# The shared key projection moved from the attention's first stage between the steps of a recurrence

## The chip, the cores and the metric

One core of a Trainium2 chip runs the whole program. Its engines work in parallel, each through its own queue in order: TensorE (PE) multiplies matrices, VectorE (DVE) and ScalarE (ACT) work on elements, GpSimd (POOL) does some of the same, SyncE (SP) mostly issues DMA transfers. ScalarE's queue issues transfers too. PSUM holds the results of TensorE, SBUF the operands, DRAM everything larger. The metric is the device time of one execution in microseconds, the median of several.

## The reference

A trunk of two layers over 2048 tokens of 1024 features. Layer 0 is a recurrence (RWKV-7) over time in 16 heads of 64. From its output, keys and values are computed once. Layer 1 is an attention with three groups of queries over these keys and values. Only the middle part changes here:

```python
xr = xr + gate * _rwkv7_time_mix(h, ...)                 # layer 0
kv = _rms(xr, kv_norm_g) @ w_kv                          # 1024 -> 2048
k_sh = kv[..., :D].reshape(B, S, N_HEADS, HEAD_DIM)
v_sh = kv[..., D:].reshape(B, S, N_HEADS, HEAD_DIM)
k_sh = _rope(_rms(k_sh, k_norm_g), cos, sin)             # norm and rotation of the keys
h = _rms(xr, b_norm_g[j]) * (1.0 + scale) + shift        # layer 1
xr = xr + gate * _dilated_mixer(h, k_sh, v_sh, ...)
```

All of it is float32.

## The kernel before

The kernel has three phases. The first (to about 1085 us) computes the projections of the recurrence. The second, called **the recurrence** here, goes over 32 chunks of 64 tokens. The third computes keys, values, queries and a gate in **jobs**, lets the attention run beside the later ones, and ends with the output projection.

A large product is made with three matmuls, because an operand in float32 is split into a high and a low half (`xh`, `xl` for tokens, `wh`, `wl` for weights): high x high, high x low, low x high. That is `mm3`, lines 72 to 74; `split` (lines 65 and 66) makes the halves of tokens, one on ScalarE and one on VectorE.

*The recurrence* (`phase2`). For each chunk, `loads` fetches the chunk's operands `ls`, `bk`, `tf`, `ut` and `x` on SP's queue (bk has one buffer), `prep` makes small triangular products from them (lines 881 to 913), and `chain` carries the state through three dependent sets of small matmuls (lines 942, 959 and 965), each of which waits for the evacuation of the one before. A chunk has ten slots; in each the program emits a step of the chain, one of `prep`, one of the chunk's normalization, and then fills from a list called `work`:

```python
fill(1, front)
fill(2 if len(work) > 1 and ch >= RUSH else 1)
```

Every block of 256 tokens (four chunks) pushes one `out_proj` onto that list: 38 steps, of which 32 hold 6 matmuls of 256 columns into the PSUM tile `pd` (192 of them), with `x1T` stored to DRAM and, at the end, the tokens' norm factor `rstd1`. `spread` ties each of these products to an earlier mark of the chain, so that a scheduler can't put them all ahead of it. The order in which each engine gets its instructions is set when the program is built, by that scheduler's own estimate of times.

*The jobs* (`phase3`, `project`). `JOBS = ("k", "v", 2, 1, 0, "gate", "out")`. A job goes over 8 blocks of 256 tokens (`tb`), and each block over 32 steps of one `mm3` with 512 columns, so 768 matmuls. `tokens` loads a tile of `x1T`, splits it, and in the value job also multiplies it by the norm (GpSimd, line 1314), modulates it (VectorE, line 1318) and stores it as `xbT` for the query jobs; the odd tiles of that job share two buffers (`yp`). `weight` loads and splits a weight tile, for keys and values with the factor `kv_norm_g` (lines 1282 and 1283). Behind every eighth step a result is taken out of PSUM: in the value job by `values_out` (scaled on ScalarE and stored), in the key and query jobs by `rotated`, which scales it on ScalarE (line 1444), norms and rotates it in `rms_rope` (VectorE lines 1205 to 1218, GpSimd lines 1207 and 1211), transposes it on PE (line 1450) and stores it, for the keys in two layouts, one of them in pieces of 64 bytes.

The attention starts when the first query job is done: `tick(256 * 3 + 14)` runs the three jobs k, v and 2 ahead of it.

## Time and profile before

| | |
|---|---|
| median of 3 runs | 3931.34 us (3910.43 to 3933.19) |
| the profiled execution | 3931.35 us, span 3929.6 us, mean granted clock 0.960 |
| PE busy | 3740.8 us, 95% of the span |
| VectorE, ScalarE, GpSimd busy | 64%, 46%, 36% |
| DMA | 595 MB, mean 151 GB/s |

The span runs from the first to the last instruction of the profile, the execution's time has a little around it. Busy shares of PE count a matmul from its start to its modelled end, and matmuls overlap, so a busy PE can still be slower than its peak. The granted clock is that of PE: 1.00 is 2.4 GHz and 0.5 is 1.2 GHz, and a figure between is a mean over a stretch.

### The profile page before, as it was taken

The numbers are of one execution on the slowest core, as the hardware profiler recorded it, in microseconds if no ns is written. First come the engines' busy times: TensorE is split into PE (matmuls) and PEld (weight loads), VectorE is DVE, ScalarE is ACT, GpSimd is POOL, SyncE is SP. The second block draws the span as 40 slices with busy tenths as digits, with TensorE's granted clock in tenths as the row PEclk, the third lists the DMA queues.
The fourth block names the chain that finished last, engine by engine and source line by source line (L and its number), as shares of the span: only waits on it lengthen the run. The fifth ranks groups of instructions, "written<-read, shape, count | busy, mean of one in ns | idle before, by whom it ended". The sixth has DMA issues, their size and how long they took to land. (4 is left out here: it accounts for less than half of the span.)

```text
span 3929.6 us, 79892 instructions
## 1 busy us (share of the span) xinstructions
PE 3740.8 (95%) x29328; PEld 2942.6 (75%) x29328; DVE 2501.7 (64%) x6212; ACT 1824.9 (46%) x4734; POOL 1430.3 (36%) x1376
## 2 busy tenths in 40 slices
PE   6899999989999999999898999899999999999999
PEld 5565667667778888888776877677777788887778
DVE  4884477989766565466575457777776654454545
ACT  4555444343334344344443233466666665564431
POOL 3341356664343344333343244533422320042232
PEclk9899999999978899899998999999999999999999
DMA  8774466675664444344588457855654455465555
GB/s 276 221 241 144 133 182 197 180 206 169 169 140 106 94 107 104 86 104 116 115 126 175 137 146 82 137 143 149 184 148 125 132 154 145 153 190 169 172 157 150
DMA packets 1027128, 595.31 MB, mean 151 GB/s; under 512 B 564912, under 2 KB 918576, under 8 KB 1020592
## 3 DMA queue, kind: packets, MB, share of 16 engines
q1 hardware_dynamic: 629040, 500.00, 45.6%
q10 hardware_dynamic: 397696, 90.20, 12.6%
q8 instruction: 232, 3.80, 0.4%
q14 instruction: 160, 1.31, 0.1%
HBM read 391.84 MB, written 198.18 MB: 150 GB/s over the span
## 5 line engine op out<-in xcount | busy, mean ns | idle before, releaser
L1645 ACT ACTIVATE yt<-yt,nm 128x256 f32<-128x256 f32 (+1 forms) x768 | 345.1, 450 | 320.0 <-DVE nm L1641 316.7
L72 PE MATMUL ps<-xh,wh 128*128 128x512 f32 (+1 forms) x1248 | 451.6, 372 | 11.5 <-ACT xh L358 7.7
L73 PE MATMUL ps<-xl,wh 128*128 128x512 f32 (+1 forms) x1248 | 449.6, 362 | 6.4 <-DVE xl L360 5.9
L74 PE MATMUL ps<-xh,wl 128*128 128x512 f32 (+1 forms) x1248 | 446.6, 359 | 0.0
L72 PE MATMUL ps<-xh 128*128 128x512 f32 (+1 forms) x1152 | 419.9, 365 | 5.9 <-ACT ov L1478 3.7
L74 PE MATMUL ps<-xh,xl 128*128 128x512 f32 (+1 forms) x1152 | 402.9, 350 | 0.0
L73 PE MATMUL ps<-xl,xh 128*128 128x512 f32 (+1 forms) x1152 | 400.9, 348 | 0.0
L1207 POOL TENSOR_TENSOR rr_st<-rr_st,mh 128x8 f32<-128x8 f32 x128 | 216.1, 1688 | 484.0 <-DVE rr_st L1206 340.6
L74 PE MATMUL ps<-wh,xl 128*128 128x512 f32 x896 | 360.2, 404 | 15.2 <-DVE xl L66 14.6
L72 PE MATMUL ps<-wh,xh 128*128 128x512 f32 x896 | 367.2, 411 | 3.4 <-ACT xh L65 1.8
L73 PE MATMUL ps<-wl,xh 128*128 128x512 f32 x896 | 359.3, 401 | 0.6 <-DVE wl L1283 0.5
L72 PEld LDWEIGHTS ps<-xh,wh 128*128 128x128 f32 x1248 | 239.4, 194 | 85.8 <-issue 34.3
L73 PEld LDWEIGHTS ps<-xl,wh 128*128 128x128 f32 x1248 | 241.7, 194 | 61.9 <-issue 19.2
L74 PEld LDWEIGHTS ps<-xh,wl 128*128 128x128 f32 x1248 | 241.8, 194 | 52.5 <-issue 21.4
L1638 DVE CUSTOM_DVE_ANT_0 yt<-sc,amask 128x256 f32<-128x256 f32 (+1 forms) x768 | 237.6, 359 | 66.3 <-PE sc L1633 60.5
L72 PEld LDWEIGHTS ps<-xh 128*128 128x128 f32 x1152 | 218.4, 190 | 54.9 <-issue 18.5
L74 PEld LDWEIGHTS ps<-xh,xl 128*128 128x128 f32 x1152 | 218.7, 190 | 29.0 <-issue 0.2
L73 PEld LDWEIGHTS ps<-xl,xh 128*128 128x128 f32 x1152 | 219.1, 190 | 25.1 <-POOL xl L1288 0.4
L1214 DVE TENSOR_TENSOR q<-rr_sq,TCS 128x256 f32<-128x256 f32 x256 | 223.4, 913 | 2.8
L1211 POOL TENSOR_TENSOR rr_a<-rr_sq,TCS 128x512 f32<-128x512 f32 x128 | 184.5, 1441 | 110.7 <-DVE rr_sq L1209 90.9
L278 DVE SCALAR_TENSOR_TENSOR t<-hx,vecs,t 128x512 f32<-128x512 f32 x192 | 169.4, 901 | 78.0 <-ACT t L277 77.6
L74 PEld LDWEIGHTS ps<-wh,xl 128*128 128x128 f32 x896 | 170.8, 191 | 62.7 <-DVE xl L66 26.5
(339 smaller groups left out, 8842.3 us busy)
## 6 DMA issues: line engine op xcount, KB each, us to landing
hx<-hT SPq DMA_DIRECT2D x152, 256.5 KB
xb<-xbT SPq DMA_DIRECT2D x256, 128.0 KB
x<-Q SPq DMA_DIRECT2D x96, 256.0 KB
kq<-K SPq DMA_DIRECT2D x72, 256.0 KB
st<-in_w_in SPq DMA_DIRECT2D x64, 256.0 KB
arD<-ar SPq DMA_DIRECT2D x32, 512.0 KB
bkD<-bk SPq DMA_DIRECT2D x32, 512.0 KB
ls<-arD SPq DMA_DIRECT2D x64, 256.0 KB
```

Of the source, the lines that this page charges most:

```text
L72: i = mm(out, lh, rh, start=first, stop=False, **kw)
L73: mm(out, lh, rl, start=False, stop=False, **kw)
L74: mm(out, ll, rh, start=False, stop=last, **kw)
L278: nc.vector.scalar_tensor_tensor(t1, hx[:, 0:512], self.vec["a_mix_mu"][:, m:m + 1], t1, op0=ALU.mult, op1=ALU.add)
L1207: nc.gpsimd.tensor_tensor(st[:, 1], st[:, 0], mh, op=ALU.pow)
L1211: nc.gpsimd.tensor_tensor(a, sq, TC[:, tt, None, :].to_broadcast([P, 8, 64]), op=ALU.mult)
L1214: nc.vector.tensor_tensor(v[:, :, lo:lo + 32], sq[:, :, hi:hi + 32], TS[:, tt, None, lo:lo + 32].to_broadcast([P, 8, 32]), op=ALU.mult)
L1638: nc.vector.tensor_tensor_reduce(out=u.pr[:, h, :nk], in0=sc[h][:, x, :nk], in1=amask[:, int(g == 0), 256 - nk:256], scale=1.0, scalar=-3e ...
L1645: nc.scalar.activation(u.pr[:, h, :nk], u.pr[:, h, :nk], AF.Exp, bias=nm[:, x, h:h + 1], accum_out=lm[:, x, h, 0:1])
```

## The change

The key job leaves the list of jobs. Its products are made in the recurrence: when an `out_proj` is done, it pushes a new generator `keys(v)` onto the same list `work`. It reads the block's 256 tokens back from `x1T`, splits them, and multiplies them by all 16 weight tiles of the keys (3 x 2 matmuls of 512 columns for each). The tiles don't stay in SBUF: the first block loads, scales and splits them and stores the halves to a DRAM scratch `wkD`; every later block reads both halves again, two tiles ahead, into three buffers. The result is scaled with `rstd1` on ScalarE and stored as `kraw`. A slot now fills two steps instead of one (three instead of two from chunk 24 on if the list is long).

In the third phase the value job comes first. Beside each of its 32 results the generator `rotated("k", ...)` now runs for the keys: it loads a tile of `kraw` in place of an evacuation and goes on as before. The value job's tokens, which were the second job's, keep their norm and modulation. The token pool of nine buffers is cut into one of five and one of four.

```diff
@@ phase2 @@
-            for n, bufs in (("wst", 2), ("dp", 1), ("op", 2)):
+            for n, bufs in (("wst", 2), ("dp", 1), ("op", 2), ("wk", 3)):
...
                 nc.gpsimd.tensor_tensor(self.rstd1[:, 2 * v:2 * v + 2], rs, mh[:, 0:2], op=ALU.pow)
+                push(keys(v))
+
+            def key_weight(v, i):
+                wh, wl = (late["wk"].tile([P, 512], F32R, name="wk" + x) for x in "hl")
+                if v:
+                    for x, t in enumerate((wh, wl)):
+                        nc.sync.dma_start(t.bitcast(F32), wkD[i, x])
+                    return lambda: (wh, wl)
+                kc, c = i % KC, i // KC * 512
+                st = late["wst"].tile([P, 512], F32, name="wst")
+                nc.sync.dma_start(st, ap["w_kv"][kc * P:(kc + 1) * P, c:c + 512])
+
+                def use():
+                    g = kvg[:, kc:kc + 1]
+                    nc.scalar.activation(wh, st, AF.Copy, scale=g)
+                    nc.vector.scalar_tensor_tensor(wl, st, g, wh.bitcast(F32), op0=ALU.mult, op1=ALU.subtract)
+                    for x, t in enumerate((wh, wl)):
+                        nc.sync.dma_start(wkD[i, x], t.bitcast(F32))
+                    return wh, wl
+                return use
+
+            def keys(v):
+                t0 = v * 256
+                xh = late["dp"].tile([P, KC, 2, P], F32R, name="yh").rearrange("p k i t -> p k (i t)")
+                xl = late["dp"].tile([P, KC, 2, P], F32R, name="yl").rearrange("p k i t -> p k (i t)")
+                uses = [key_weight(v, i) for i in range(2)]
+                for kc in range(0, KC, 4):
+                    nc.sync.dma_start(xl[:, kc:kc + 4].bitcast(F32),
+                                      self.x1T[kc * P:kc * P + 512, t0:t0 + 256].rearrange("(k p) t -> p k t", p=P))
+                yield
+                yield
+                for kc in range(0, KC, 2):
+                    q = slice(kc, kc + 2)
+                    raw = xl[:, q].bitcast(F32)
+                    nc.scalar.activation(xh[:, q], raw, AF.Copy)
+                    yielding(nc.vector.tensor_sub(xl[:, q], raw, xh[:, q].bitcast(F32)))
+                    yield
+                for half in range(2):
+                    ps = [late["pd"].tile([P, 512], F32, name="pd") for _ in range(2)]
+                    for kc in range(KC):
+                        i = half * KC + kc
+                        w = uses.pop(0)()
+                        if i + 2 < 2 * KC:
+                            uses.append(key_weight(v, i + 2))
+                        for b in range(2):
+                            c = slice(b * P, b * P + P)
+                            spread(self.mm3(ps[b], (xh[:, kc, c], xl[:, kc, c]), w, kc == 0, kc == KC - 1))
+                            yield
+                    for b in range(2):
+                        o = late["wst"].tile([P, 512], F32, name="wst")
+                        nc.scalar.activation(o, ps[b], AF.Copy, scale=self.rstd1[:, 2 * v + b:2 * v + b + 1])
+                        nc.sync.dma_start(self.kraw[t0 + b * P:t0 + b * P + P, half * 512:half * 512 + 512], o)
+                    yield
...
-                fill(2 if len(work) > 1 and ch >= RUSH else 1)
+                fill(3 if len(work) > 1 and ch >= RUSH else 2)
@@ phase3 @@
-            JOBS = ("k", "v", 2, 1, 0, "gate", "out")
+            JOBS = ("v", 2, 1, 0, "gate", "out")
...
+                if job == "k":
+                    nc.sync.dma_start(q, self.kraw[tt * P:tt * P + P, half * 512:half * 512 + 512].rearrange(
+                        "t (h c) -> t h c", c=64))
+                    for _ in range(4):
+                        yield
+                else:
+                    nc.scalar.activation(q, ps.rearrange("p (h c) -> p h c", c=64), AF.Copy)
...
+                        if job == "v" and kc == 0:
+                            after.append(rotated("k", tb * 2 + i, half, None))
...
-            tick(256 * 3 + 14)
+            tick(256 * 2 + 14)
```

The scheduler sets where the moved instructions stand. Counted in PE's order, the extra products of the four chunks of a block were 72, 60, 60 and none of 256 columns; in the changed kernel's steady pattern they are 120 of 256 columns, then 24 and 18 of 512, then 48 of 512, then 30 of 512 and 48 of 256. Behind the last chunk stand 252 of 256 columns before, and 192 of 256 with 174 of 512 now, the latter in part among 30 of the value job's.

PE's queue in the recurrence before, in a chunk without extra products, from the end of one block's norm on (`ls` and `tf` are operands of the chunk, `qc` an evacuated step of the chain, `bk` the next chunk's operand):

```order
L1093 MATMUL pd<-ones,acc 128x2 x2
L959 MATMUL ps<-qc_15992,tf_10366 64x64 x8
L881 MATMUL z<-ls_0_10355,bk 128x128 x4
L942 MATMUL ps<-x,ls_1_10362 64x64
L944 MATMUL y<-x,ls_1_10362 64x64
L942 MATMUL ps<-x,ls_1_10362 64x64 x7
```

The same place in the changed kernel (`wkh`, `wkl` are the halves of a key weight tile, `yh`, `yl` those of the tokens):

```order
L967 MATMUL ps<-x,ls_15454 64x64 x8
L1095 MATMUL pd<-ones,acc 128x2 x2
L969 MATMUL y<-x,ls_15454 64x64 x8
L72 MATMUL pd<-wkh,yh 128x512
L73 MATMUL pd<-wkl,yh 128x512
L74 MATMUL pd<-wkh,yl 128x512
```

Products of 512 columns follow where the chain's next set stood.

SP's queue in the recurrence before, loads of the next chunk (`x`, `ls`, `tf`) between those of the output projection:

```order
L1082 DMA x1T<-t_18533 128x256
L859 DMA tf_10359<-tdD 32x8x32 x4
L1074 DMA t_18995<-in_xT 128x256
L865 DMA x<-vP 64x512 x2
L850 DMA ls_1_10362<-arD 64x8x128 x2
```

In the changed kernel, while a block's keys are made:

```order
L867 DMA x<-vP 64x512 x2
L1108 DMA wkl<-wkD 128x512
L1108 DMA wkh<-wkD 128x512
L1154 DMA kraw<-wst 128x512
L852 DMA ls_0_10360<-arD 64x8x128
```

The load of `ls` now stands behind two weight halves and a store of finished keys.

VectorE's queue in the value job before (token splits on line 66, modulation on line 1318, weight halves on line 1288):

```order
L66 TENSOR_TENSOR xl<-yc,xh 128x256
L66 TENSOR_TENSOR xl<-xb,xh 128x256
L1318 TENSOR_SCALAR xb<-xb,gsB,adaB 128x256
L1318 TENSOR_SCALAR yc<-yc,gsB,adaB 128x256
L1288 TENSOR_TENSOR wl<-st,wh 128x512 x3
```

In the changed kernel (the modulation is now on line 1380, the keys' norm and rotation on lines 1264 to 1277):

```order
L1273 TENSOR_TENSOR q<-rr_sq,TCS 128x8x32 x2
L1277 TENSOR_TENSOR rr_a<-rr_a,q 128x512
L66 TENSOR_TENSOR xl<-yc,xh 128x256
L66 TENSOR_TENSOR xl<-xb,xh 128x256
L1264 TENSOR_REDUCE rr_st<-rr_sq 128x8
```

The splits now take turns with the rotation's instructions.

## Rows read from the trace of the kernel before

**Rows 1.** The page: busy us, share, instructions by engine; GB/s of 40 slices

```profile
PE 3740.8 (95%) x29328; PEld 2942.6 (75%) x29328; DVE 2501.7 (64%) x6212; ACT 1824.9 (46%) x4734; POOL 1430.3 (36%) x1376
...
GB/s 276 221 241 144 133 182 197 180 206 169 169 140 106 94 107 104 86 104 116 115 126 175 137 146 82 137 143 149 184 148 125 132 154 145 153 190 169 172 157 150
```

**Rows 2.** Windows: length; busy PE, PEld, DVE, ACT, POOL; clock, DMA share, GB/s

```profile
1840.00:1902.00 62.00, 50.78 (x341) 45.09 (x342) 30.29 (x66) 27.98 (x59) 15.84 (x16) 0.93 0.55 171
1902.00:2112.00 210.00, 196.01 (x875) 155.13 (x875) 154.21 (x273) 100.07 (x196) 105.07 (x69) 0.97 0.81 129
2112.00:2315.00 203.00, 191.51 (x822) 154.55 (x821) 82.22 (x145) 62.61 (x132) 58.65 (x68) 0.97 0.57 165
2315.00:2520.00 205.00, 192.30 (x869) 148.93 (x868) 151.35 (x254) 81.15 (x169) 106.11 (x69) 1.00 0.71 93
1085.00:1840.00 755.00, 723.87 (x10147) 630.74 (x10147) 443.54 (x1342) 310.60 (x856) 292.61 (x335) 0.90 0.44 102
...
900.00:1000.00 100.00, 97.06 (x769) 72.25 (x767) 90.56 (x172) 41.83 (x76) 36.09 (x53) 0.95 0.71 203
```

**Rows 3.** Same view: single chunks, then twenty together

```profile
1404.50:1419.10 14.60, 13.41 (x237) 11.78 (x236) 12.06 (x40) 6.49 (x19) 6.97 (x8) 1.00 0.57 122
...
1783.40:1800.20 16.80, 14.04 (x245) 12.26 (x244) 12.65 (x40) 8.06 (x24) 7.68 (x8) 1.00 0.50 108
1444.40:1466.60 22.20, 22.20 (x333) 19.74 (x332) 14.19 (x46) 8.94 (x26) 8.93 (x10) 1.00 0.43 93
...
1759.90:1783.40 23.50, 23.50 (x343) 20.67 (x342) 12.50 (x36) 9.74 (x28) 8.83 (x10) 1.00 0.41 96
1419.10:1444.40 25.30, 25.30 (x360) 22.24 (x354) 16.35 (x46) 12.03 (x33) 10.10 (x12) 1.00 0.45 107
1800.20:1826.50 26.30, 26.25 (x386) 23.04 (x386) 16.52 (x45) 12.14 (x32) 10.79 (x11) 1.00 0.26 64
1329.50:1800.20 470.70, 454.81 (x6546) 399.62 (x6544) 270.36 (x832) 195.63 (x544) 179.56 (x199) 0.94 0.42 100
```

**Rows 4.** Same view, instructions of the tile pd alone

```profile
1444.40:1466.60 22.20, 9.66 (x61) 7.71 (x60) 1.43 (x3) 0.00 (x0) 1.00 0.43 93
```

**Rows 5.** Timeline of PE: start, us, engine, line, operation

```profile
1838.07 0.28 PE L72 MATMUL pd<-yh,wh 128*128 128x256 f32 x1
1838.19 0.28 PE L73 MATMUL pd<-yl,wh 128*128 128x256 f32 x1
...
2200.14 0.39 PE L73 MATMUL ps<-wl,xh 128*128 128x512 f32 x1
2200.36 0.39 PE L74 MATMUL ps<-wh,xl 128*128 128x512 f32 x1
```

**Rows 6.** Busy time by window, as in rows 2

```profile
1495.00:1500.00 5.00, 2.92 (x50) 2.56 (x46) 4.64 (x16) 0.76 (x2) 3.64 (x6) 1.00 0.80 157
...
1505.00:1511.00 6.00, 6.00 (x56) 5.32 (x54) 2.10 (x6) 2.46 (x8) 1.22 (x2) 0.50 0.64 132
...
1651.00:1655.00 4.00, 4.00 (x34) 3.54 (x33) 1.35 (x4) 3.31 (x10) 0.00 (x0) 0.50 0.17 56
```

**Rows 7.** Waits from 1400 to 1600 us: total, times, longest

```profile
PE z L881 <- DMA bk<-bkD: 5.2, 3, 2.1
```

**Rows 8.** Groups by line: four of the key job, two of the value job

```profile
L1214 DVE TENSOR_TENSOR q<-rr_sq,TCS 128x256 f32<-128x256 f32 x62 | 54.7, 922 | 0.6
L1209 DVE TENSOR_TENSOR rr_sq<-q,rr_st 128x512 f32<-128x512 f32 x32 | 23.2, 725 | 46.8 <-POOL rr_st L1207 46.8
L66 DVE TENSOR_TENSOR xl<-xb,xh 128x256 fp32r<-128x256 f32 x59 | 22.8, 415 | 1.1 <-ACT xh L65 1.1
...
L1444 ACT ACTIVATE q<-ps,rstd 128x512 f32<-128x512 f32 x32 | 21.8, 684 | 21.6 <-PE ps L74 9.9 <-DVE rr_st L1205 4.4 <-DVE rr_a L1218 2.4
...
L66 DVE TENSOR_TENSOR xl<-xb,xh 128x256 fp32r<-128x256 f32 x37 | 24.0, 653 | 5.4 <-ACT xh L65 5.1
...
L1214 DVE TENSOR_TENSOR q<-rr_sq,TCS 128x256 f32<-128x256 f32 x2 | 0.7, 410 | 0.0
```

More of the change, by code (lines that the diff above doesn't have):

```diff
@@ L1169, in phase2 @@
             cctx.close()
-            for n, bufs in (("wst", 3), ("wp0", 9), ("xb", 5), ("xs", 9)):
+            for n, bufs in (("wst", 3), ("wp0", 9), ("xb", 5), ("xs", 5)):
                 self.kept[n] = pool(n, bufs, keep)
@@ L1236, in phase3 @@
             wst, pp, pt, xb_, xp = (kept[n] for n in ("wst", "pp", "pt", "xb", "xs"))
+            xps = [xp] * 5 + [pool("xs1", 4)] * 4
             wp, ep = (kept["wp0"], self.xp0), pool("ep", 1)
@@ L1273, in weight @@
                 st = wst.tile([P, 512], F32, name="st")
-                w = ap["w_kv"] if job in ("k", "v") else ap["b_w_out"][0] if job == "out" else ap["b_w_in"][0]
-                c = (3 if job == "gate" else {"k": 0, "v": 1, "out": 0}.get(job, job)) * D + half * 512
+                w = ap["w_kv"] if job == "v" else ap["b_w_out"][0] if job == "out" else ap["b_w_in"][0]
+                c = (3 if job == "gate" else {"v": 1, "out": 0}.get(job, job)) * D + half * 512
                 nc.sync.dma_start(st, w[kc * P:(kc + 1) * P, c:c + 512])
@@ L1279, in use @@
                     wh, wl = (wp[half].tile([P, 512], F32R, name="wx"[half] + x) for x in "hl")
-                    if job in ("k", "v"):
+                    if job == "v":
                         g = self.vec["kv_norm_g"][:, kc:kc + 1]
@@ L1304, in tokens @@
                     return merge(tb, kc, rows, sl, halves)
-                if p == 1 and kc % 2:
+                if p == 0 and kc % 2:
                     xb = two("yp")[:, 0]
@@ L1440, in phase3, with rotated @@
             pairs = {}
-            def rotated(job, tt, half, ps, scale):
+            def rotated(job, tt, half, ps):
                 q = s3.tile([P, 8, 64], F32, name="q")
-                nc.scalar.activation(q, ps.rearrange("p (h c) -> p h c", c=64), AF.Copy, scale=scale)
+                if job == "k":
[5 more added lines that the diff above has]
+                    nc.scalar.activation(q, ps.rearrange("p (h c) -> p h c", c=64), AF.Copy)
                 yield
@@ L1507, in project @@
             def project():
+                rstd(0)
                 for kc in range(KC):
-                    w, x = weight("k", 0, kc), tokens(0, kc)
+                    w, x = weight("v", 0, kc), tokens(0, kc)
                     w(), x()
@@ L1554, in project @@
                             after.append(gate(tb, gi, ps) if job == "gate" else values_out(*a) if job == "v" else
-                                         result(tb, gi, ps) if job == "out" else
-                                         rotated(job, *a, self.rstd1[:, a[0]:a[0] + 1] if job == "k" else 1.0))
+                                         result(tb, gi, ps) if job == "out" else rotated(job, *a))
                         if n >= 8 * OUT - 1 and s >= 24:
```

15 lines of the change are left out of this document (10 added, 5 removed).

## The prediction

> **What bounds the kernel now.** The page comes first: TensorE (PE) is busy for 95% of the span, no other engine for more than 64% [rows 1]. That alone says little, because an idle-looking engine can still set a stage's pace, so I next cut the span into stages with the view of busy time by window [rows 2]: the recurrence (1085 to 1840 us), the key job (1902 to 2112), the value job (2112 to 2315) and the first query job behind it. The reader is to see that the change takes one whole stage, the key job of 210 us, out of a part where PE is busy 93% of the time, and puts its products into a stage of 755 us where PE is busy 96% of the time at a mean granted clock of 0.90.
>
> So the question is whether the recurrence has gaps on PE that work from elsewhere can fill. The recurrence's chunks answer it. The output projection is already spread between its steps, but unevenly: of every four chunks, one gets 72 of its products, two get 60 and one gets none (this repeats from the seventh chunk on; a chunk of 60 stands in [rows 4], where one matmul more belongs to a small sum). At full clock a chunk without them takes 14.6 to 16.8 us (three such, mean 15.6); a chunk with 60 takes 22.2 to 23.5 (three, mean 22.8); one with 72 takes 25.3 and 26.3, mean 25.8 [rows 3], where the shortest and the longest of each kind stand in that order. Products of 256 columns follow each other every 0.12 us [rows 5]: 60 of them are 7.2 us, 72 are 8.6 us. The chunk grew by 7.2 us for 7.2 us of work and by 10.2 us for 8.6. Over four chunks that is 24.6 us for 23.0, a factor of 1.07. **Work put between the steps is not hidden; it is paid for in full.** In the chunks with 60, PE is busy for every microsecond of the window; even in those without any it is busy for 84 to 92% of it [rows 3].
>
> **What is moved, and what it costs.** The key product is 8 token blocks x 96 matmuls of 512 columns, 768 in all, in both kernels. Such matmuls follow each other every 0.23 us [rows 5], so 768 x 0.231 = 177 us. In the recurrence I charge them at the measured factor: 177 x 1.07 = **+190 us**. The order of PE's queue shows where they stand: in the steady pattern four chunks get 45 us of extra products in place of 23, and none is empty any more. A quarter of them (174 of 768) comes behind the last chunk, partly between the first value products; these are no cheaper and no dearer.
>
> **What may come back there.** The five groups of four chunks from 1329.5 to 1800.2 us take 94.1 us each [rows 3], and 15.6 + 2 x 22.8 + 25.8 = 87.0 us at full clock. The other 7 us per group are waits and half clock: from 1495 to 1500 us PE idled for 2, and from 1505 to 1511 it ran at the lower of its two levels (0.5, which is 1.2 GHz) although it was busy throughout [rows 6]. Behind such idling stands the load of the next chunk's bk, which has one buffer: PE waits for it by name for 5.2 us in 200, up to 2.1 at a time [rows 7]. Longer chunks leave that load more time, so some of it should go. Seven groups at 7 us bound the gain at 50 us; the bound below is nothing. I take **-15**, nearer to nothing, because the change puts more loads on the same queue.
>
> **The streamed weights.** Each of the 8 blocks reads all 16 key weight tiles again, two halves of 256 KB each: 8.4 MB per block, on SP's queue, three buffers deep. The trace of before has no such stream. Best rates of a slice are 276 GB/s, the recurrence runs at 102 [rows 1, 2]: one pair of 512 KB takes 1.9 us at the one and 5.1 at the other. PE uses a pair in 6 x 0.231 = 1.4 us when pairs come back to back, and about every 3.4 us on average (16 pairs in some 55 of 110 us), with a lead of two pairs. So the stream keeps up on average, and not where two pairs stand in a row, which the order shows in several places. No wait at all is 0 us; every second of the 128 pairs late by 1.25 us is 80. I take **+20**, because the average fits. SP runs in order: behind a weight load that waits for its buffer, or a store of finished keys that waits for ScalarE, stand the loads of the next chunk (x, ls, bk), so a delay here reaches the chain twice.
>
> **The end of the recurrence.** The last block's keys need x1 that has just been stored and is read back. Before, the stretch from 1840 to 1902 us holds 51 us of busy PE in 62 [rows 2]; the remaining keys of the seventh block and 30 value products now fill some of the gaps, and the read-back opens one. **+4** (0 to 12). What ScalarE and VectorE get in the recurrence (per block four splits, four evictions) costs nothing there: they are busy for 41% and 59% of it [rows 2]. If that cover were gone, 8 x 4 evictions of 0.68 us as in the key job [rows 8] would be 22 us.
>
> **The value job, with the keys' norm and rotation in it.** Before, the two jobs take 210 + 203 = 413 us [rows 2]. PE alone needs 210 for the joint one: that is the key job, with the same 768 products and the 128 transposes of the keys. VectorE had 154 us of work in the one and 82 in the other [rows 2]; one of the two sets of token splits (64 x 0.41 = 26 us [rows 8]) and of the key weights' low halves (5 us) go, which leaves 205. The highest VectorE share in any 100 us of this trace is 0.906 [rows 2]; 205 / 0.906 = 226 us. Its queue is in order, and the order shows the splits on which PE waits standing behind the rotation's instructions. The token loads add a little: the odd ones share two buffers, which a chain through GpSimd, VectorE and a store has to free. I take **235**, with 210 and 275 as ends (the upper one is worked out under the rivals). The gain is 413 - 235 = **-178 us**. GpSimd's 105 + 59 us fit in 235. The stores of both jobs now share one stage; their DMA shares add up to 0.81 + 0.57 [rows 2], and what late landings do is in the 9 us between 226 and 235.
>
> Edits with one answer: the token pool split in two of five and four buffers keeps nine in all, and the shift of the attention's start from three jobs to two follows the jobs; neither costs anything as long as the query jobs follow at 205 us as before [rows 2].
>
> **Sum**, against the profiled execution's own 3931.35 us (span 3929.6), which is also the median: 190 - 15 + 20 + 4 - 178 = +21. **Forecast: 3952 us**, no measurable change. About 1% (39 us) is what a measurement of this kernel can tell from no change.
>
> **Rivals.** *The recurrence does absorb part of it* (faster): no chunk is empty, PE never idles for 2 us, the clock stays at its upper level and bk is always there. Then 190 - 50 + 0 + 4, and the value job is at PE's 210: -203. Sum -59, **3872 us**. For it: the clock was lost in an empty chunk. Against it: it was also low from 1651 to 1655, inside a chunk that holds 60 of the products [rows 6], and the factor of 1.07 was measured at full clock.
>
> *The weight stream stalls PE* (slower): every burst of pairs waits, SP is held and bk comes later than before, so that the half clock stays too. 190 + 0 + 80 + 10 - 178 = +102, **4033 us**. It decides from the point where a pair takes longer to arrive than the two ahead of it last, 2.8 us in a burst.
>
> *VectorE and GpSimd block each other in the value job* (slower): the trace has signs of it. The rotation's half products take 0.92 us each in the key job and 0.41 where GpSimd is quiet; splits take 0.42 there and 0.65 in the value job beside GpSimd's products [rows 8]. If the two never overlap, VectorE's instructions with two inputs in SBUF cost at their unhindered price 64 x 0.41 for the half products, 64 x 0.73 for the two full ones (the price of the first), 64 x 0.42 for the splits and 10 for weights, 110 us, beside GpSimd's 105 + 59 = 164 [rows 2]: 274, say 275. Sum: 190 - 15 + 20 + 4 - 138 = +61, **3992 us**. It decides once these two sums together pass PE's 210. The Trainium skill ("SBUF — State Buffer", section "SBUF: two separate sides") states such a rule: the port pair that the two share is an exclusive lock, held for a whole instruction, against VectorE's instructions with two SBUF inputs. By that rule the 275 stands; the trace agrees only in part, since VectorE's and GpSimd's busy times of the key job (154 + 105) already exceed its 210 us.
>
> *The change doesn't do what it says:* keys could pile up behind the recurrence. The order speaks against it, three quarters are inside, and since PE pays either way the time would be that of the forecast.
>
> **How the numbers follow.** The forecast has 0.48 (its own range 3905 to 3990), the faster rival 0.14, the stream 0.18, the lock 0.20. The 8-in-10 range cuts some of the faster rival and of the stream's far end: 3885 to 4035. Faster by over 1% (below 3892) is nearly all of the faster rival: 0.14. Slower by over 1% (above 3970) is the stream, most of the lock and the upper edge of the forecast: 0.40. The rest, 0.46, is within 1%.
>
> **What would show it.** In the changed kernel's profile: four chunks of the recurrence together at 105 to 120 us instead of 94; PE without idle windows there; waits of PE for the weight halves below 30 us in all; one value job of 225 to 250 us with VectorE above 80%; the query job behind it at 205. The prediction is wrong if four chunks stay below 100 us (the recurrence had room), if PE's waits for weights pass 60 us, or if the value job takes over 265 us.

## The result and the profile after

The changed kernel takes 3995.1 us (median of 4, 3983.2 to 4006.8) against 3932.3 beside it (4, 3910.4 to 3950.9): a ratio of 1.0156, interval 1.0117 to 1.0194, so 1.6% **slower** by 63 us, where the forecast was +21. The profiled execution took 4004.98 us, span 4003.2, which is 73.6 more than that of before.

The page first, busy us and GB/s by slice as in [rows 1]:

```profile
PE 3737.0 (93%) x29328; PEld 2908.6 (73%) x29328; DVE 2500.3 (62%) x6180; ACT 1812.8 (45%) x4702; POOL 1439.3 (36%) x1376
...
GB/s 271 226 234 149 134 186 178 191 183 206 154 129 129 208 184 183 194 179 183 194 197 160 175 203 77 120 138 154 184 149 128 117 168 141 156 183 171 172 154 144
```

No engine has more to do than before but GpSimd, whose 1376 instructions took 9 us more; PE is busy for 4 us less. The recurrence's slices (the 12th to the 20th) now move 129 to 208 GB/s. The time went into waiting. Two marks in the trace cut it into three parts: the end of the last matmul into `pd` (before at 1898.6, after at 2069.9 us) and the start of the last eviction of values (2307.6 and 2355.6). The recurrence, with the products behind its last chunk, grew by 171.3 us, the jobs of keys and values shrank from 409.0 to 285.7, so by 123.3, and what follows grew from 1622.0 to 1647.6, by 25.6. 171.3 - 123.3 + 25.6 = 73.6.

Windows of the changed kernel, columns as in [rows 2]: the whole recurrence, the stretch of [rows 3]'s last row, two stretches of about four chunks, one with and one without half clock, 10 us of half clock, the value job, and 205 us behind it:

```profile
1085.00:2069.90 984.90, 918.44 (x11242) 763.78 (x11241) 510.67 (x1456) 380.44 (x987) 314.09 (x355) 0.93 0.66 178
1329.50:1800.20 470.70, 450.84 (x5782) 372.84 (x5782) 243.02 (x711) 184.02 (x491) 151.16 (x165) 0.96 0.69 184
1444.00:1553.40 109.40, 104.91 (x1394) 87.53 (x1393) 57.36 (x166) 42.84 (x115) 36.44 (x40) 0.97 0.67 179
1759.20:1769.40 10.20, 8.45 (x34) 6.31 (x34) 1.67 (x5) 3.92 (x11) 1.69 (x2) 0.50 0.47 154
1810.50:1916.40 105.90, 102.82 (x1399) 86.31 (x1398) 58.01 (x169) 43.09 (x116) 36.42 (x40) 1.00 0.69 187
2069.90:2355.60 285.70, 215.77 (x891) 166.81 (x891) 185.44 (x321) 97.28 (x202) 154.09 (x125) 0.89 0.86 178
2355.60:2560.60 205.00, 189.47 (x837) 149.58 (x836) 139.76 (x243) 80.00 (x165) 96.59 (x63) 0.95 0.76 104
```

In the recurrence four chunks take 105.9 to 112.9 us from the fifteenth chunk on (126 in the two groups ahead of it) instead of 94.1, and the transfer engines' share has risen from 0.42 to 0.69. In the value job PE is busy for 216 of 286 us (76%), VectorE for 65%, ScalarE for 34%: no engine is near its limit, and the clock is 0.89. What holds it must then be waits of the engines for each other, and the waits of that window show which (engine and line, what it waited for, us in total, times, longest):

```profile
PE tr L1518 <- ACT of L1538: 26.2, 6, 10.2
PE ps L72 <- ACT ov L1546: 26.1, 8, 8.2
PE ps L72 <- ACT xh L65: 13.1, 7, 4.4
...
DVE xl L66 <- ACT xh L65: 33.5, 16, 4.9
...
DVE rr_st L1264 <- ACT rr_sq L1261: 26.3, 7, 6.5
...
ACT xh L65 <- issue: 20.9, 4, 6.6
```

PE and VectorE wait for ScalarE, which is the least busy of the five. What it does instead stands in the timeline of its queue (start, us, engine, line, operation; ACTq is its sequencer, which issues the transfers):

```profile
2213.27 0.33 ACTq L1382 DMA_DIRECT2D xbT<-yc  x1
2213.69 0.39 ACTq L1532 DMA_DIRECT2D K<-sg  x1
2214.12 0.64 ACTq L1541 DMA_DIRECT2D K<-of  x1
2214.86 5.77 ACTq L1382 DMA_DIRECT2D xbT<-xb  x1
2220.72 0.60 ACT L1526 ACTIVATE sg<-tr 128x512 f32<-128x512 f32 x1 [8.41 <-DMA yc<-x1T]
```

An issue takes 0.33 to 0.64 us, and the one behind the store `K<-of` takes 5.77. That store is the transposed copy of the keys (`K2`, line 1541): 512 KB in 8192 pieces of 64 bytes. Until the issue is through, the activations behind it in the queue stand, those on which PE waits among them. It happens behind each of the 14 such stores that fall into the value job: the next issue, whenever it starts, is through 6.1 to 9.6 us after the store. 15 issues of the job take over 1 us, 72.0 us together. In the kernel before there are 7 over both jobs, 23.8 us. There the next issue behind 13 of the 16 stores was the plain copy of the keys, 4.2 to 9.1 us later, so that little or nothing was left to stand for (at most 2.81 us); the last three stores were followed by stores of tokens or values and cost 5.31, 4.63 and 6.91 us. One of each kind, before:

```profile
1947.41 0.52 ACTq L1473 DMA_DIRECT2D K<-of  x1
1953.51 0.71 ACTq L1464 DMA_DIRECT2D K<-sg  x1
...
2097.91 0.70 ACTq L1473 DMA_DIRECT2D K<-of  x1
2101.43 5.31 ACTq L1320 DMA_DIRECT2D xbT<-xb  x1
```

### The profile page after: what moved, and what is told of

The parts are those of the page before. It is cut to its first block, busy times and chain, and to the rows that moved or that the text cites. A ratio compares the mean times of both kernels' runs of the same rounds, so it can differ in the third digit from the quotient of the medians.

```text
span 4003.2 us, 80119 instructions
## 1 busy us (share of the span) xinstructions
PE 3737.0 (93%) x29328; PEld 2908.6 (73%) x29328; DVE 2500.3 (62%) x6180; ACT 1812.8 (45%) x4702; POOL 1439.3 (36%) x1376
## 5 line engine op out<-in xcount | busy, mean ns | idle before, releaser
L72 PE MATMUL ps<-xh 128*128 128x512 f32 (+1 forms) x1024 | 371.6, 364 | 29.5 <-ACT ov L1546 21.3
L73 PE MATMUL ps<-xl,xh 128*128 128x512 f32 (+1 forms) x1024 | 354.4, 346 | 3.1 <-POOL xl L1348 2.0
L74 PE MATMUL ps<-xh,xl 128*128 128x512 f32 (+1 forms) x1024 | 354.1, 346 | 0.0
L72 PE MATMUL ps<-wh,xh 128*128 128x512 f32 x768 | 323.1, 421 | 19.4 <-ACT xh L65 13.1
L74 PE MATMUL ps<-wh,xl 128*128 128x512 f32 x768 | 310.8, 409 | 8.7 <-DVE xl L66 8.3
L73 PE MATMUL ps<-wl,xh 128*128 128x512 f32 x768 | 313.5, 408 | 0.0
L72 PEld LDWEIGHTS ps<-xh 128*128 128x128 f32 x1024 | 196.6, 192 | 74.7 <-ACT ov L1546 23.3
L73 PEld LDWEIGHTS ps<-xl,xh 128*128 128x128 f32 x1024 | 197.4, 193 | 24.4 <-POOL xl L1348 3.3
L74 PEld LDWEIGHTS ps<-xh,xl 128*128 128x128 f32 x1024 | 196.4, 192 | 23.0 <-issue 0.2
L1703 PE MATMUL sc<-kq,x 64*128 64x256 f32 (+1 forms) x1536 | 206.2, 359 | 2.4 <-DVE lm L1708 2.1
```

The costliest lines, as they stand in the source:

```text
L72: i = mm(out, lh, rh, start=first, stop=False, **kw)
L73: mm(out, lh, rl, start=False, stop=False, **kw)
L74: mm(out, ll, rh, start=False, stop=last, **kw)
L1703: j = mm(sc[h][:, x, :u.n * P], qt[r, c], kq[r, k1 - u.n * P:k1], start=True, stop=True)
```

## The experiments

**Theory A**: in the value job ScalarE's queue is held by the issues behind the stores of small pieces. **Rival B**: GpSimd's products and VectorE shut each other out. For the recurrence: **P**, the products of the keys themselves cost what it lost, against **S**, the streamed weights do. The table has all runs. Columns: the end of the last matmul into `pd`; from there to the last eviction of values; the issues of over 1 us on ScalarE's queue in that job, summed; median and number of executions; ratio to the kernel before with its interval. The first three are from the one profiled execution.

| run | recurrence ends | value job | long issues | total us (n) | ratio |
|---|---|---|---|---|---|
| before | 1898.6 | 409.0 (two jobs) | 23.8 | 3932.3 (4) | |
| after | 2069.9 | 285.7 | 72.0 | 3995.1 (4) | 1.0156 (1.0117 to 1.0194) |
| e1_long_runs | 2080.8 | 240.0 | 0.0 | 3934.6 (10) | 0.9971 (0.9938 to 1.0003) |
| e2_four_pieces | 2060.0 | 281.7 | 74.9 | 3977.7 (8) | 1.0095 (1.0062 to 1.0128) |
| e3_no_norm_on_gpsimd | 2062.3 | 242.2 | 57.2 | 3980.1 (1) | |
| e4_a_third | 2125.4 | 270.6 | 57.0 | 4037.7 (1) | |
| e5_no_stream | 2015.1 | 284.3 | 61.4 | 3929.9 (1) | |
| e9_third_no_stream | 1982.5 | 267.6 | 53.9 | 3887.3 (1) | |
| e8_sp_stores | 2089.0 | 247.1 | 42.1 | 3950.4 (10) | 1.0033 (0.9998 to 1.0069) |
| e10_runs_of_128 | 2077.1 | 284.7 | 51.9 | 3982.0 (4) | 1.0115 (1.0064 to 1.0166) |
| f1_four_pairs | 2028.7 | 278.6 | 59.1 | 3948.1 (10) | 1.0026 (1.0003 to 1.0049) |
| f2_product_on_vector | 2063.8 | 262.7 | 71.9 | 3963.0 (1) | |
| f3_three_together | 2041.9 | 245.2 | 19.2 | 3917.0 (7) | 0.9937 (0.9907 to 0.9967) |
| f4_all_four | 2032.2 | 246.8 | 16.7 | 3908.1 (7) | 0.9918 (0.9887 to 0.9949) |

How much one execution scatters can be read from it: where nothing of the recurrence is edited (after, e1, e2, e3, e8, e10, f2) it ends between 2060.0 and 2089.0, mean 2071.8; where nothing of the value job's work is edited (after, e4, e5, e9, f1) that job takes 268 to 286. Differences inside these bands say nothing; the changed kernel's own profile is at the upper end of the second, so gains of the value job that are counted from its 285.7 are at the high side. Totals of one execution alone are weak: the changed kernel's four lie between 3983.2 and 4006.8. The kernel before had medians of 3932 to 3946 beside the runs, so that the plain differences of medians given below are 3 to 12 us smaller than those of the ratios.

### The value job

**e1_long_runs.** The transposed copy of the keys is written in the plain order of the tokens, in runs of 1 KB (its contents are then in the wrong places for the attention).

```diff
-  nc.scalar.dma_start(dst.rearrange("p j (r t i) -> p t (j r) i", r=16, i=16)[:, tt // 2], ...)
+  nc.scalar.dma_start(dst[:, :, tt // 2 * 256:tt // 2 * 256 + 256], o2)      # keys only
```

> Changed kernel, with the keys' second layout stored in runs of 1 KB in place of pieces of 64 bytes: the same bytes, a sixteenth of the packets. The second layout's content is therefore in another order, so what the attention reads from it is not the reference's. Theory A (the store in 64-byte pieces fills ScalarE's transfer queue and blocks ScalarE's next issue for 5 to 6 us, 16 times): issues of over 1 us on ScalarE's queue fall from 77 us to under 15, and the value job (last pd matmul to last value eviction) from 286 us to 215 to 240; the total falls by 50 to 110 us. Theory B (VectorE and GpSimd lock each other): the value job stays within 15 us of 286. Theory C (the bytes of both jobs' stores are too many for the DMA engines): it stays above 260.

The long issues are gone, all 133 are below 1 us, and the value job takes 240.0 us; the total falls by 60. The timeline of ScalarE, an issue beside an activation at the usual price, and the window of the value job:

```profile
2214.70 0.60 ACT L1526 ACTIVATE sg<-tr 128x512 f32<-128x512 f32 x1
2214.76 0.33 ACTq L1550 DMA_DIRECT2D V<-ov  x1
2215.20 0.60 ACT L1538 ACTIVATE of<-tr 128x512 f32<-128x512 f32 x1
```

```profile
2080.80:2320.80 240.00, 202.90 (x879) 159.22 (x880) 181.63 (x320) 98.39 (x202) 151.63 (x125) 0.95 0.67 214
```

VectorE's and GpSimd's work is the same as in the changed kernel (182 and 152 us of 240), so nothing of rival B is touched, and the 46 us (28 from the low end of the band) come from the small pieces. Whether they act by the queue or by the load of their packets on the transfer engines (their share is 0.67 here, 0.86 in the changed kernel) this run doesn't say; e8 does.

**e2_four_pieces.** Each such store is cut into four, two steps of the job apart.

```diff
+  for j in range(4):
+      nc.scalar.dma_start(d16[:, j], s16[:, j])      # one of four heads' columns
+      yield
+      yield
```

> Changed kernel, with each store of the keys' second layout cut into four, one every two steps of the job; same packets, computes the reference's result. Theory A: the queue no longer fills in one go, blocked issues fall from 77 us to under 40 and the value job from 286 to 230 to 260 us, the total by 30 to 80 us. If the sum of the packets is what counts (theory C), the value job stays above 275. Theory B: within 15 us of 286.

The time at issues is the same, 74.9 us, in 39 issues instead of 15, and so is the job; the total is 17 us lower, with intervals that overlap. Theory A had expected less than 40 us. It is not the size of one store that counts; the number of pieces in the queue as a whole would fit, but no run varies that alone.

**e8_sp_stores.** The values and the modulated tokens are stored from SyncE's queue.

```diff
-  nc.scalar.dma_start(xbT[rows, sl], xb)
+  nc.sync.dma_start(xbT[rows, sl], xb)
-  nc.scalar.dma_start(V[tt * P:(tt + 1) * P, half * 512:half * 512 + 512], o)
+  nc.sync.dma_start(V[tt * P:(tt + 1) * P, half * 512:half * 512 + 512], o)
```

> V and the modulated tokens are stored from SyncE's queue, so that only the key stores are issued by ScalarE. If the value job is held by ScalarE standing at the issue behind a store of 64-byte pieces, its blocked time falls from 72 us to under 25, the value job from 286 us to 240 to 255 and the total by 25 to 45 us, to 3950 to 3970. If the stores' packets themselves or GpSimd's product hold it, the job stays above 270 us and the total within 15 us of 3995; if SyncE's queue now waits for the evictions with the loads behind them, it is slower than 4000.

The value job falls to 247.1 us and the total by 45, with no change in what is transferred: the queue, not the bandwidth, was the price. The block itself fell only to 42.1 us, not under 25: `K<-sg`, the plain copy of the keys, is still issued behind `K<-of`, 2 to 10 us after it (median 4, where the next issue came after a median of 2 in the changed kernel), so that only a little less is left to stand for. The window:

```profile
2089.00:2336.10 247.10, 207.41 (x897) 162.97 (x896) 187.95 (x320) 97.87 (x202) 150.97 (x124) 0.94 0.96 204
```

The transfer engines' share is 0.96 there, against 0.86 in the changed kernel: the bytes are the same and the job is shorter. The Trainium skill ("DMA: Bandwidth & Descriptors", section "Rules for kernel authors") says that spreading transfers over the issuing engines brings no bandwidth and only saves time of the sequencer that issues. The saving of issuing time is what this run shows, and it was worth 39 us of the job.

**e10_runs_of_128.** The keys are rotated in another order, four token tiles of one half of the heads after another, so that eight stores of 128-byte pieces take the place of sixteen of 64.

```diff
-  after.append(rotated("k", tb * 2 + i, half, None))
+  m = 4 * tb + gi
+  after.append(rotated("k", m // 8 * 4 + m % 4, m // 4 % 2, None))
-  ... dst.rearrange("p j (r t i) -> p t (j r) i", r=16, i=16)[:, tt // 2]      # every second tile
+  ... K2[half].rearrange("p j (r t i) -> p t (j r) i", r=16, i=32)[:, tt // 4] # every fourth
```

> The keys are rotated four token tiles of one half of the heads after another, so that the transposed copy is stored in half as many pieces, of 128 bytes (8 stores for 16), all from ScalarE as before. If the number of pieces sets the block, ScalarE's blocked time halves to about 36 us, the value job falls by some 20 us to 265 and the total to 3965 to 3978. If each store blocks the same whatever its pieces, it is also halved; if only the bytes count, nothing changes (3995).

Inconclusive by itself. There are 7 long issues instead of 15, but each lasts longer, up to

```profile
2236.49 11.18 ACTq L1556 DMA_DIRECT2D V<-ov  x1
```

so that 51.9 us remain, and the job is no shorter. Half the pieces took away 28% of the block, not half. Whether that is the bytes of a piece or the new order of the rotations, no run tells; in runs of 1 KB the same bytes left no block at all.

**e3_no_norm_on_gpsimd.** GpSimd's product of tokens and norm factor in the value job is left out.

```diff
   if p == 0:
-      nc.gpsimd.tensor_tensor(xb, xb, rb[tb], op=ALU.mult)
       later(2, modulated)
```

> Changed kernel without GpSimd's product of the tokens with their norm in the value job (line 1376): the tokens for the query jobs are left unnormed, all else stays. It takes 64 instructions, some 50 us, from GpSimd. Theory B (lock): the value job shrinks by 25 us or more from 286. Theory A: by less than 10 us, blocked issues stay near 77 us.

This speaks against A alone: the value job also falls to 242.2 us, with 57.2 us of long issues still in it. Either relief, this one or that of e1, is enough for a job of some 240, so the two prices overlap and don't add up. Its total fell by only 15, because the part behind the job took 1673.5 us where it takes 1620 to 1648 in the other runs named here; for that this one execution gives no reason.

**f2_product_on_vector.** The same product goes to VectorE.

```diff
-  nc.gpsimd.tensor_tensor(xb, xb, rb[tb], op=ALU.mult)
+  nc.vector.tensor_tensor(xb, xb, rb[tb], op=ALU.mult)
```

> The tokens' norm product in the value job goes from GpSimd to VectorE, with everything else as in the changed kernel. Without that product the value job took 242 us instead of 286. If GpSimd's work shuts VectorE out, the product costs VectorE some 64 x 0.35 us = 22 us and gives the lock back: value job 245 to 265. If the product's place in the chain of the stores alone counted, 270 to 290; the total is 3970 to 3985 in the first case, 3985 to 4005 in the second.

262.7 us for the job with all of the block still there, 5 us below the band of one execution, so the product on GpSimd probably costs some of it. Whether by the lock or by its place in the chain, a look at prices gives a size: in the changed kernel's value job VectorE's half products, splits and modulations take

```profile
L1273 DVE TENSOR_TENSOR q<-rr_sq,TCS 128x256 f32<-128x256 f32 x63 | 37.4, 632 | 0.5
L66 DVE TENSOR_TENSOR xl<-xb,xh 128x256 fp32r<-128x256 f32 x34 | 19.8, 584 | 3.8 <-ACT xh L65 3.8
L1380 DVE TENSOR_SCALAR yc<-yc,gsB,adaB 128x256 f32<-128x256 f32 x30 | 20.8, 696 | 1.3 <-POOL yc L1376 1.3
L1380 DVE TENSOR_SCALAR xb<-xb,gsB,adaB 128x256 f32<-128x256 f32 x29 | 15.8, 545 | 0.0
```

and with GpSimd's product left out:

```profile
L1273 DVE TENSOR_TENSOR q<-rr_sq,TCS 128x256 f32<-128x256 f32 x54 | 26.8, 536 | 0.6
L66 DVE TENSOR_TENSOR xl<-xb,xh 128x256 fp32r<-128x256 f32 x35 | 16.7, 480 | 6.3 <-ACT xh L65 6.2
L1379 DVE TENSOR_SCALAR yc<-yc,gsB,adaB 128x256 f32<-128x256 f32 x30 | 14.1, 471 | 0.1
L1379 DVE TENSOR_SCALAR xb<-xb,gsB,adaB 128x256 f32<-128x256 f32 x29 | 11.8, 407 | 0.1
```

The half products cost 63 x 0.096 = 6 us more, the splits of both kinds 5, and the modulations, which have one operand of this size and stand in no rival of the prediction, 30 x 0.225 + 29 x 0.138 = 11. With all rows of the two views it is some 25 us of hindrance on an engine that is 65% busy: rival B is there, but it is not what sets 286. The rest of what e3 and f2 gave back may be the chain from load to store, which frees the buffers; that is argued, no run isolates it.

### The recurrence

Where its 171 us stand shows in three stretches: up to the fifteenth chunk, the 16 chunks from there on, and the rest. The first and the last hold the products of two blocks of keys each, the middle those of four. Lengths in us (with the clock) from the one profiled execution:

| kernel | first | middle | last |
|---|---|---|---|
| before | 334.1 (0.85) | 381.1 (0.93) | 98.4 (0.97) |
| after | 392.7 (0.87) | 438.7 (0.97) | 153.5 (0.93) |
| e5_no_stream | 378.6 (0.87) | 415.7 (0.99) | 135.8 (0.96) |
| e9_third_no_stream | 388.6 (0.81) | 383.3 (0.98) | 125.6 (0.93) |
| f1_four_pairs | 367.6 (0.92) | 429.3 (0.98) | 146.8 (0.95) |

It is 58.6, 57.6 and 55.1 us from before to after: the middle, with half of the products, has a third of the loss. In the seven kernels whose recurrence isn't edited the middle takes 437 to 451 us. One more thing changes beside the edits: where the scheduler puts the products. In e4, e5, e9, f1, f3 and f4 it deals them out otherwise (in e5 and with four pairs 57, 15, 168 and 48 in four chunks where it was 48, 78, 120 and 42, counted in the trace), and no run gives one of these edits without that.

**e4_a_third.** The keys' product is cut to its high by high part, 256 matmuls for 768.

```diff
-  spread(self.mm3(ps[b], (xh[:, kc, c], xl[:, kc, c]), w, kc == 0, kc == KC - 1))
+  spread(mm(ps[b], xh[:, kc, c], w[0], start=kc == 0, stop=kc == KC - 1))
```

> Changed kernel with the key product in the recurrence from high x high alone (one matmul in place of three; the two products with low halves are left out, the weight stream, splits, evictions and stores stay). 512 matmuls of 0.231 us fewer, 118 us. Work between the steps is paid in full: four chunks in steady state fall from 110-113 us by 14 to 16 us, to 95 to 98, the stretch to the last pd matmul by 95 to 125 us. Rival (the recurrence absorbs it and the stream, or the chain, sets the pace): four chunks fall by under 5 us.

A third of the work made the recurrence **longer**, by 56 us; neither theory had that. Four chunks took some 119 to 140 us. Its window and PE's waits from 1300 us on:

```profile
1085.00:2125.40 1040.40, 932.09 (x10703) 774.99 (x10701) 501.35 (x1440) 379.41 (x984) 309.58 (x341) 0.79 0.65 168
```

```profile
PE pd L1149 <- DMA wkh<-wkD: 23.5, 20, 5.7
PE z L883 <- DMA bk<-bkD: 13.3, 9, 2.2
```

The clock is 0.79 instead of 0.93. PE uses up a pair in a third of the time and waits for the next. From 1290 us on the trace has 25 stretches at half clock; each begins in or just behind an idle gap of PE of over 0.5 us, 13 of them at a wait for weights or for `bk`, the others at other waits.

**e5_no_stream.** Blocks after the first load two pairs of weights and use them for all 16 steps.

```diff
-  w = uses.pop(0)()
-  if i + 2 < 2 * KC:
+  if i < 2 or not v:
+      held[i % 2] = uses.pop(0)()
+  w = held[i % 2]
+  if i + 2 < 2 * KC and not v:
       uses.append(key_weight(v, i + 2))
```

> Blocks after the first load two pairs of key weights once and use them for all 16 steps (the keys come from the wrong weights; the matmuls, splits, evictions and stores all stay). If the matmuls alone set the price of the recurrence, chunks 14 to 29 keep some 110 us per four and the last block's tail shrinks by its waits for weights only (about 15 us): total 3980 to 3995. If the streamed weights cost more than those waits (contention with the loads of the recurrence, a lower clock), the groups of four fall to 95 to 103 us and the total to 3940 to 3960.

The second case: 3929.9 us. The last four groups of four chunks take 102.1, 103.6, 104.7 and 105.3 us, the recurrence ends 57 us before the mean of the kernels with the stream, and the clock is higher:

```profile
1085.00:2015.10 930.10, 882.75 (x11241) 748.40 (x11239) 499.71 (x1454) 379.34 (x986) 314.53 (x354) 0.94 0.53 133
```

The same number of matmuls (11241) in 55 us less, 23 of them in the middle. So S holds for 55 us, the other deal of the products included, although PE waits for the weights by name for only 15.4 us in all. Of the 55, 19 are idle time of PE, and in 36 it was busy for longer over the same matmuls, of which the clock (0.93 for 0.94) explains less than half.

**e9_third_no_stream.** Both edits at once.

> The keys' product is cut to its high by high part and the weights are not streamed (keys wrong). The third alone made four chunks take 118 to 140 us at a clock of 0.65 to 0.82. If a stream that PE outran caused that, it is gone here and four chunks take 90 to 98 us, the total is some 3900 to 3930. If the clock fell because TensorE had less to do between the steps, the groups stay above 110 us and the clock below 0.85, total above 3980.

97.8, 94.6, 97.4 and 93.4 us for four chunks, 3887.3 us in all: less work alone was not what made e4 slow; it took the stream beside it. Beside e5 it also prices the products: 512 matmuls are 2015.1 - 1982.5 = 32.6 us, 0.064 each, where they follow each other every 0.23 us; two single executions, whose scatter (29 us from the lowest to the highest of seven) is nearly as large. In the middle the first third costs nothing that can be seen, 383.3 us against 381.1 before. But the recurrence as a whole is still 84 us longer than before, 55 in the first stretch, where the first block also loads, scales, splits and stores the weights, and 27 in the last. No run takes these apart.

**f1_four_pairs.** Four buffers for the pairs of weights instead of three; the value job's token halves begin with three buffers instead of five, nine in all as before.

```diff
-  (("wst", 2), ("dp", 1), ("op", 2), ("wk", 3))
+  (("wst", 2), ("dp", 1), ("op", 2), ("wk", 4))
-  (("wst", 3), ("wp0", 9), ("xb", 5), ("xs", 5))
+  (("wst", 3), ("wp0", 9), ("xb", 5), ("xs", 3))
-  xps = [xp] * 5 + [pool("xs1", 4)] * 4
+  xps = [xp] * 3 + [pool("xs1", 6)] * 6
```

> Four buffers for the pairs of key weights instead of three (the value job's token halves give two of their early buffers for it), so that SyncE no longer waits for the matmuls of the step just queued before it goes on to the recurrence's loads. If the stream's price (the 65 us that went without it) is SyncE's queue standing, its wait there (87 us of 500) falls below 30, four chunks take 104 to 107 us instead of 110 and the total is 3950 to 3980. If it is the load on the transfer engines, the groups and the total stay within 15 us of 3995.

3948.1 us, 47 less, with every byte of the stream still there: for these 47 the bytes are not what costs. The recurrence ends at 2028.7, in f3 and f4, which have the fourth pair too, at 2041.9 and 2032.2. SyncE's queue changed as expected. Its waits from 1400 to 1900 us, after:

```profile
SPq L1108 <- PE pd L74: 67.5, 47, 4.7
...
SPq L1108 <- PE pd L73: 19.8, 6, 5.7
```

and with four pairs:

```profile
SPq L1108 <- PE pd L74: 43.7, 37, 3.5
```

Line 1108 loads a pair. With three, SyncE stands until the matmuls of the step just queued are done, 87 us of 500; with four 44 (not below 30, as expected). The loads of `bk` and `ls` behind it come earlier in this window: PE's wait at line 883 falls from

```profile
PE z L883 <- DMA bk<-bkD: 10.1, 10, 3.6
```

to

```profile
PE z L883 <- DMA bk<-bkD: 3.5, 6, 1.2
```

But this is not where most of the gain stands. Four chunks take 103.6 to 111.2 us, mean 107.3, against 109.7 in the changed kernel (104 to 107 was expected): the middle gained 9 of the 41 us, the first stretch 25 (22 in the mean of f1, f3 and f4 against the seven). And over the whole recurrence PE waits for `bk` no less with four pairs than with three. Three:

```profile
PE z L883 <- DMA bk<-bkD: 14.6, 15, 3.6
```

Four:

```profile
PE z L883 <- DMA bk<-bkD: 17.0, 15, 4.0
```

What differs over the whole is the busy time and the clock, here with four pairs, beside 918.44 and 0.93:

```profile
1085.00:2028.70 943.70, 882.00 (x11207) 742.85 (x11206) 494.80 (x1439) 380.18 (x982) 307.94 (x342) 0.95 0.69 184
```

36 of the 41 us are PE being busy for less time over the same work, 5 are idle time. That the recurrence is shorter with a fourth pair is measured three times, by 30 to 43 us against the mean of the seven; that this comes by SyncE's queue and `bk` is shown for a small part only, in the middle.

A gap can cost more than itself. In the changed kernel PE idles for 3.63 us at 1757.3, waiting for `bk`, and from 1759.2 to 1769.4 the clock is at its lower level (window above); of the four stretches of half clock between 1450 and 1900 us three follow a gap at this line. Other gaps at it, of 0.92 us at 1568.9 and 0.57 at 1869.9, were not followed by one. What share of the gain belongs to the other deal of the products stays open.

### A version that beats both

**f3_three_together** has e8, e10 and f1 in one kernel; **f4_all_four** adds f2.

> V and the modulated tokens stored from SyncE, the keys' copy in pieces of 128 bytes, four pairs of key weights. If the gains add up (45 by the queue, 10 by the pieces, 15 to 40 by the fourth pair), 3895 to 3930, which is faster than the kernel before. If the value job is by then held by its own work, 3930 to 3955, no different from the kernel before.

> The three changes of the run before (stores from SyncE, pieces of 128 bytes, four pairs of key weights) and the tokens' norm product on VectorE. If that product still holds the value job when ScalarE is free, the job falls from 245 us to 225 to 235 and the total to 3892 to 3908. If VectorE, with 64 products more, is now the bound, the job stays at 240 to 250 and the total at 3910 to 3925.

f3 is 0.6% and f4 0.8% faster than the kernel before, 78 and 87 us faster than the changed one. Most of the gains of queue and fourth pair add up (45 + 47, with e10's 13 it is 105, of which 78 came); the product on VectorE adds nothing to the value job once ScalarE is free (246.8 for 245.2 us), which fits that what f2 had given back was slack behind the same block. Between f3 and f4 the intervals overlap. The value job of f4:

```profile
2032.20:2279.00 246.80, 207.40 (x896) 161.87 (x896) 187.31 (x389) 100.10 (x206) 110.90 (x68) 0.94 0.80 210
```

PE 84%, VectorE 76%, clock 0.94: the 37 us above PE's 210 are waits that no run here took away.

## Why the prediction was right or wrong

The measured 3995 lies in the range of 3885 to 4035, but the likeliest case, +21 and no measurable change, did not come; it is slower by more than 1%, which had a chance of 0.40. That the range held is in part luck: against the forecast the recurrence came out 28 us shorter, the step from two jobs to one 55 dearer and what follows 26 longer, together the 53 us between +21 and +73.6.

**The step that failed is the value job's size.** The prediction took 235 us, from VectorE at 0.906 of its time, and put what the stores of both jobs do to each other into "the 9 us between 226 and 235". Measured: 285.7. By the prediction's own mark (over 265) that is wrong. VectorE was at 65%, so it was not the bound at all; its 205 us of work were 185. The stores were: 72 us of ScalarE's queue at a standstill behind pieces of 64 bytes; with long runs in their place (e1) the job took 240.0. They held it together with the way through GpSimd's product, without which (e3) it took 242.2 with most of the standstill left. Without that block the estimate of 235 was near, though not for its reason: VectorE was at 76% in e1, not at 91%. The number of pieces and the queue that issues them stand in the code and in the trace of before (an issue of 5.31 us at 2101.43, in the key job); the prediction looked at the transfers' share and not at the issues. The key job alone bore them, since for its first 13 stores nothing was issued behind them for 4.2 us or more.

**"The query job behind it at 205"**: what follows the value job took 25.6 us longer. The last block's keys are still being stored when the next job begins (two of the 16 stores come behind the last eviction of values); its third result comes 41.3 us after the last eviction of values, where it was 13.0 before.

**The recurrence**: +199 was forecast (190 - 15 + 20 + 4), +171.3 came, and two errors in it cancel. "Paid for in full", at a factor of 1.07, was too dear: without the stream the same products cost 2015.1 - 1898.6 = 116.5 us instead of 179. In the middle stretch, where 4 x 96 x 0.231 = 89 us of products were added, e5 is only 34.6 us longer than before. The waits gave nothing back there, PE idles for 14.1 us in both. The clock did, 0.93 to 0.99, some 23 us (0.07 of 381.1 less 0.01 of 415.7); the other 31 us were found in time that had counted as busy, and how is open. Over the whole recurrence before, the clock is low:

```profile
1085.00:1898.60 813.60, 773.32 (x10484) 674.68 (x10483) 473.61 (x1406) 335.86 (x910) 307.74 (x350) 0.90 0.45 107
```

The streamed weights were put at 20 and cost 55, the new deal of the products included; the first block makes its weights, so the pairs read back are 112 and not the 128 of the prediction's upper bound. The mechanism in the text (SyncE in order, the next chunk's loads behind a weight load that waits for its buffer) is there in SyncE's waits, but its price was taken from how often PE would wait for weights, and most of the 55 us are in no named wait. The mark "below 30 us of waits for the weights" was met at 15.4 and proved nothing. By stretches the prediction's 190 are 47, 95 and 47, with its 4 for the end in the last; measured, with the stream, came 58.6, 57.6 and 55.1. The middle, from which the factor was read, was put much too dear, the ends were not.

**The rivals.** "The weight stream stalls PE" had the right place and a third of the path right: of its 80 us 55 came with the stream, 15.4 of them at most as pairs that arrive late. "VectorE and GpSimd block each other" gave 275 us for the job and 3992 in all, near the measured 286 and 3995, but that is luck: with both engines' work untouched e1 took 240, less than the 275 below which the two could not get if they never overlapped. What they cost each other is, by the prices above, some 25 us of VectorE's time. "The recurrence absorbs part" was true of a part of the products, as e5 and e9 show, and hidden under the stream. That the change does what it says was right: no chunk is empty and the key job is gone.

## What to carry to other kernels

Before moving a job onto another, count for each queue the transfers that it issues and the pieces that each has: here a store of 8192 pieces of 64 bytes held the next issue of its queue until 6 to 10 us after it, and cost next to nothing as long as nothing was issued in that time. Don't price a stream by the consumer's waits for it alone: here these were 15 us, and without the stream the recurrence was 55 shorter. Try a buffer more before giving up; it gave back 47 us with the same traffic, and by which path stays in part open. When no engine of a stage is near its limit, as in this value job with 76% at most, look for the least busy engine that the others wait for, and then at its issues.

## What the hardware showed unexpectedly

- Cutting the matmuls that fill the recurrence to a third, with the stream kept, made it 56 us longer in the one execution taken: the clock fell from 0.93 to 0.79.
- The issue behind a store of 8192 pieces of 64 bytes took up to 7.6 us on ScalarE's queue, behind one of as many pieces of 128 bytes up to 11.2, behind 1 KB runs of the same bytes always below 1; the usual issue takes 0.33 to 0.4.
- Four pieces of such a store, apart from each other, cost the queue 75 us, where whole ones cost 72.
- One more buffer for a pair of weights made the recurrence 41 us shorter, although PE waited for its other operand `bk` for 17.0 us instead of 14.6.
